# Down pass of a hybrid decoder trunk: later loads ordered behind one-column copies, first product's weights staged in the two general slots

## The chip, the cores and the metric

The kernel runs on one core of one Trainium2 chip. The metric is the device time of one execution in microseconds (us). The time before is 2121.87 us, the median of 3 runs (2121.12 to 2127.75). The engines are called by name: TensorE (PE; its weight loads are PEld), VectorE (DVE), ScalarE (ACT), GpSimd (POOL) and SyncE (SP). The last two issue most of the DMA loads and stores; SP also has "SPq", its queue, in the profile.

## The reference

Two residual layers over 1024 positions of width 1024. The first mixes with causal differential attention and causal pooling, the second with sliding-window attention; each ends with a gated MLP, and that is the part the change is in:

```python
def conv_glu_ffn(x, norm_g, w_up, conv_w, conv_b, w_down):
    S = x.shape[1]
    h = rms_norm(x, norm_g) @ w_up
    hp = jnp.pad(h, ((0, 0), (CONV_W - 1, 0), (0, 0)))
    c = conv_b
    for j in range(CONV_W):
        c = c + conv_w[j] * hp[:, j:j + S]
    gate, up = jnp.split(c, 2, axis=-1)
    return x + (jax.nn.silu(gate) * up) @ w_down
```

`w_down` is 2816 x 1024 in each layer. All inputs and outputs are float32.

## The kernel before

The activations are kept transposed (features on the 128 partitions, positions along the free side). For each layer the MLP has two passes. The **up pass** (`ffn_up`) computes the gated values for 22 blocks of 128 features and stores each block to a DRAM buffer `gd` (L393). The **down pass** (`ffn_down`, L547) reads `gd` back and multiplies it by `w_down`. It runs twice in the program, once in each layer.

The down pass is a product of 2 x 2 blocks done with seven block products instead of eight, in the order 1, 5, 6, 3, 7, 2, 4. Each product has K = 11 steps; a step is named (p, k), and `seq` (L554) lists them. A step takes a pair of operands, one of weights and one of `gd` values or sums of these. Each operand is split in a rounded high part (ScalarE, L131) and the rest (VectorE, L132), and a step is 4 x 3 = 12 matmuls of 128 x 512 (L634) into four PSUM banks. After the last step of each product VectorE adds the banks to the residual tiles `x` (L656).

A step's work is spread over three moments, counted in steps ahead of its matmuls. `fetch` (FETCH = 14 ahead) loads the weights from DRAM on SyncE's queue into staging tiles: two steps' worth in one load of 512 KB for products 1, 6, 3, 2 and 4 (L571), two loads of 256 KB for each step of products 5 and 7 (L578). `gather` (LEAD = 8 ahead) forms sums and differences on VectorE (L592). `prepare` (AHEAD = 3 ahead) splits both operands into `ws` tiles, of which there are 8, so four steps' operands.

The staging tiles come from pools with few slots: `wr` has 2, `x` has 8, `r` has 3. The `wr` and `x` slots are used by the up pass as well, and the 8 residual tiles of the down pass also live in `x` slots. The tiles `r` and `b` (11 of them) live in memory that the up pass used for other tiles. The table `stages` says which slots a product's loads take in turn. Before the change product 1, with 6 loads, takes `wr, wr, x, x, x, x`, and product 5 takes `r, wr, r, wr, r` in rotation.

The `gd` values come on GpSimd's queue. `b1` (4 tiles, L584) holds rows for the first EARLY = 4 steps of product 1; `b11` holds the others, and later all of them. The left half of each `b` tile is `b11[k]`, the right half `b21[k]`; the left and right halves of the tiles `cc`, which take `xg` slots, are `b12[k]` and `b22[k]`. The loads of `b11` (L673 for k of 4 and more, L676 for the first four), `b12` (L677), the residual `x` (L680), `b22` (L682) and `b21` (L684) are all written out before the first product. A tile framework orders the instructions of each engine by priority with a simulated timeline of its own, and puts in the semaphore waits that the tiles' uses demand; each engine and each queue then runs its instructions in that order.

Of the kernel before, what the change touches and what calls it, by code (L numbers as in the profile page):

```python
# [13 lines left out]
F32 = mybir.dt.float32  # L14
F32R = mybir.dt.float32r
I32 = mybir.dt.int32
AF = mybir.ActivationFunctionType
# [3 lines left out]
P = 128  # L21
D = 1024
S = 1024
ND = D // P
# [31 lines left out]
LO_OUT = 0  # L56
EARLY = 4
AHEAD = 3
LEAD = 8
FETCH = 14  # L60

PAR_NORM = 0
PAR_AQ, PAR_AK, PAR_SUB, PAR_CQ, PAR_CK = 32, 33, 34, 35, 36
# [5 lines left out]
class Trunk:  # L69
# [477 lines left out]
    def ffn_down(self, layer, xs, gd, after, begin=lambda part: None):  # L547

        nc, I = self.nc, self.I
        w = I["w_down"][layer]  # L550
        K = NF // 2
        lo, hi = slice(0, HALF), slice(HALF, S)
# [2 lines left out]
        pairs = {1: (0, lo), 6: (0, lo), 3: (K, lo), 2: (K, lo), 4: (K, hi)}  # L555
        raws, parts, ops = {}, {}, {}
        stages = {p: ("r", "wr", "r", "wr", "r") for p in (5, 6, 3, 7, 2)}
        stages[1], stages[4] = ("wr", "wr", "x", "x", "x", "x"), ("r",)
        taken = dict.fromkeys(stages, 0)

        def stage(p):
            t = self.big(stages[p][taken[p] % len(stages[p])], F32, HL)
            taken[p] += 1
            return t

        def fetch(p, k):
            if p in pairs:
                if k % 2 == 0:
                    t, n = stage(p), min(2, K - k)
                    off, cols = pairs[p]  # L570
                    nc.sync.dma_start(  # L571
                        t[:, :n, :], w[off + k:off + k + n, :, cols].rearrange("i p c -> p i c"))
                    raws[p, k], raws[p, k + 1] = t[:, 0, :], t[:, 1, :]
                return
            t = stage(p)
            first, second = ((k, hi), (K + k, hi)) if p == 5 else ((k, lo), (k, hi))
            for n, (row, cols) in enumerate((first, second)):
                nc.sync.dma_start(t[:, n, :], w[row, :, cols])  # L578
            raws[p, k] = t[:, 0, :], t[:, 1, :]

        g = lambda i, cols: gd[i * P:(i + 1) * P, cols]
# [5 lines left out]
        b11, b21 = [t[:, lo] for t in bb], [t[:, hi] for t in bb]  # L587
        b12, b22 = [t[:, lo] for t in cc], [t[:, hi] for t in cc]
# [6 lines left out]
        def operand(src):  # L595
            op = self.big("ws", F32R, HL)
            self.split2(src, op)
            return op

        def gather(p, k):  # L600
            r = raws.pop((p, k))
            with self.urgent(9000):
                if p == 1:
                    l, m = r, b1[k][:] if k < EARLY else b11[k]
                elif p == 5:
                    l = combine(sums[k], r[0], r[1], ALU.add)
                    m = combine(b11[k], b12[k], b11[k])
                elif p == 6:
                    l = combine(sums[k], sums[k], r)
                    m = combine(b11[k], b22[k], b11[k])  # L610
                elif p == 3:
                    l, m = combine(sums[k], r, sums[k]), b22[k]
                elif p == 7:
                    l = combine(r[0], r[0], r[1])
                    m = combine(b22[k], b22[k], b12[k])
                elif p == 2:
                    l, m = r, b21[k]
                else:
                    l, m = r, combine(b21[k], b21[k], b11[k])
            parts[p, k] = l, m  # L620

        def prepare(p, k):
            l, m = parts.pop((p, k))
            with self.urgent(12000):
                ops[p, k] = operand(l), operand(m)

        banks = {}

# [33 lines left out]
        def lead(n):  # L662
            if n + FETCH < len(seq):
                fetch(*seq[n + FETCH])
            if n + LEAD < len(seq):
                gather(*seq[n + LEAD])
            if n + AHEAD < len(seq):
                prepare(*seq[n + AHEAD])

        for n in range(FETCH):  # L670
            fetch(*seq[n])
        for k in range(EARLY, K):
            nc.gpsimd.dma_start(b11[k], g(k, hi))  # L673
        for k in range(K):
            if k < EARLY:
                nc.gpsimd.dma_start(b11[k], g(k, hi))  # L676
            nc.gpsimd.dma_start(b12[k], g(k, lo))  # L677
        x = [self.big("x") for _ in range(ND)]
        for d in range(ND):
            nc.gpsimd.dma_start(x[d][:], xs[d * P:(d + 1) * P, :])  # L680
        for k in range(K):
            nc.gpsimd.dma_start(b22[k], g(K + k, lo))  # L682
        for k in range(K):
            nc.gpsimd.dma_start(b21[k], g(K + k, hi))  # L684
        for n in range(LEAD):
            gather(*seq[n])
        for n in range(AHEAD):
            prepare(*seq[n])
# [755 lines left out]
```

## Time and profile before

| | |
|---|---|
| time, median of 3 runs | 2121.87 us (2121.12 to 2127.75) |
| profiled execution, its own time | 2124.41 us |
| span of its trace, first to last instruction | 2122.2 us |
| busy, share of the span: TensorE, its weight loads, VectorE, ScalarE, GpSimd | 95%, 81%, 75%, 52%, 12% |
| matmuls of the down passes (L634) | 1848 records in the trace |
| first and last of them | 850.8 us, 2117.7 us |
| DMA | 216.97 MB, 102 GB/s over the span |

The profile divides the span into 40 slices of 53 us; a digit is a busy share in tenths. The time of the trace counts from its first instruction. Matmuls overlap, so the duration of one (about 390 ns) is longer than the distance from one to the next. For an idle stretch the trace names what ended it, and "landing" of a DMA is the time from its issue until its data are in.

### The profile page before, as it was taken

Reading aid. Unit: us, or ns where it says so; the run is one execution under the profiler, and the core shown is the slowest. Engines: PE = TensorE matmul, PEld = TensorE weight load, DVE = VectorE, ACT = ScalarE, POOL = GpSimd, SP = SyncE. Lnnn points to the kernel's source line nnn. Section 1 sums busy time; section 2 is a strip of 40 time slices with the busy share of each in tenths; the row PEclk is TensorE's granted clock in tenths of the full one; section 3 lists DMA queues with packets and bytes.
Section 4 is the critical chain, followed back from the end, with each engine's and each line's share of the span. In section 5 each row is a group of like instructions: output and inputs, shape, how many; then the busy total and the mean of one; then the engine's idle time right before and its main releaser. Section 6 shows DMA issues by size and latency. Waiting matters only on the chain.

```text
span 2122.2 us, 28436 instructions
## 1 busy us (share of the span) xinstructions
PE 2016.3 (95%) x10440; PEld 1719.0 (81%) x10440; DVE 1602.0 (75%) x2882; ACT 1107.2 (52%) x2115; POOL 257.8 (12%) x449
## 2 busy tenths in 40 slices
PE   8999999889999999699999989999999999979999
PEld 6999877677888888588789988777788888867887
DVE  6677787877787777598863887777978777758975
ACT  5476755444455554345454875654645455433443
POOL 0322452000000002300013321200000000031000
PEclk9999999999999999899999999999999999999999
DMA  4210121302212224763431101212221222268342
GB/s 170 90 49 23 64 95 61 119 30 90 90 70 86 84 90 164 275 217 105 144 115 40 51 21 50 73 58 80 92 87 70 80 90 90 89 229 312 100 164 85
DMA packets 82333, 216.97 MB, mean 102 GB/s; under 512 B 9361, under 2 KB 9873, under 8 KB 82193
## 3 DMA queue, kind: packets, MB, share of 16 engines
q1 hardware_dynamic: 65296, 169.00, 23.0%
q0 software_dynamic: 9984, 33.56, 4.3%
q10 hardware_dynamic: 6912, 12.59, 1.6%
q8 instruction: 82, 1.34, 0.3%
q14 instruction: 59, 0.48, 0.1%
HBM read 173.17 MB, written 41.94 MB: 101 GB/s over the span
## 4 chain that ended last, share of the span: by engine, by line
PE 82%; DVE 7%; ACT 4%; DMA 3%; issue 2%; POOL 1%; SPq 0%; ACTq 0%; DVEq 0%; POOLq 0%
PE pss L372 22%; PE psq L372 12%; PE pss L634 7%; PE psq L634 6%; PE psd L720 6%; PE psd L123 5%; PE psd L372 5%; PE psd L634 4%; PE pss L720 3%; PE psq L123 2%; PE psq L893 1%; DMA b<-gd 1%; PE pss L945 1%; PE pss L791 1%; PE pss L792 1%
## 5 line engine op out<-in xcount | busy, mean ns | idle before, releaser
L372 PE MATMUL pss<-xg,ws 128*128 128x512 f32 x1248 | 297.0, 391 | 10.8 <-DVE xg L132 6.1
L372 PEld LDWEIGHTS pss<-xg,ws 128*128 128x128 f32 x1248 | 234.5, 189 | 62.3 <-DVE xg L132 7.0
L634 PE MATMUL pss<-ws,ws 128*128 128x512 f32 x726 | 209.5, 398 | 34.3 <-ACT ws L131 27.0
L372 PE MATMUL pss<-T,ws 128*128 128x512 f32 x912 | 224.6, 390 | 3.4 <-ACT ws L131 3.4
L372 PEld LDWEIGHTS pss<-T,ws 128*128 128x128 f32 x912 | 171.1, 188 | 39.6 <-ACT ws L131 4.2
L634 PEld LDWEIGHTS pss<-ws,ws 128*128 128x128 f32 x726 | 138.0, 192 | 66.1 <-ACT ws L131 27.9
L634 PE MATMUL psq<-ws,ws 128*128 128x512 f32 x660 | 191.5, 393 | 0.0
L720 PE MATMUL psd<-ws,xg 128*128 128x256 f32 x1344 | 184.0, 285 | 2.2 <-DVE hms L729 1.7
L720 PEld LDWEIGHTS psd<-ws,xg 128*128 128x128 f32 x1344 | 171.5, 191 | 4.7 <-DVE hms L729 2.3
L372 PE MATMUL psq<-xg,ws 128*128 128x512 f32 x696 | 168.5, 391 | 0.0
L132 DVE TENSOR_TENSOR ws<-hf,ws 128x512 fp32r<-128x512 f32 x160 | 109.6, 689 | 73.4 <-ACT ws L131 73.1
L372 PEld LDWEIGHTS psq<-xg,ws 128*128 128x128 f32 x696 | 131.1, 188 | 27.2
L131 ACT ACTIVATE ws<-wr 128x512 fp32r<-128x512 f32 (+1 forms) x156 | 114.2, 737 | 68.9 <-PE pss L372 23.7
L634 PEld LDWEIGHTS psq<-ws,ws 128*128 128x128 f32 x660 | 125.4, 190 | 26.4
L634 PE MATMUL psd<-ws,ws 128*128 128x512 f32 x462 | 145.6, 397 | 0.8 <-DVE ms L242 0.8
L123 PE MATMUL psd<-xg,ws 128*128 128x512 f32 x528 | 140.2, 404 | 3.1 <-DVE x L272 2.3
L131 ACT ACTIVATE ws<-hf 128x512 fp32r<-128x512 f32 x160 | 100.0, 630 | 76.1 <-PE psq L372 33.3
L677 POOL DMA_DIRECT2D xg<-gd x22 | 12.1, 552 | 988.8 <-PE pss L372 961.0
L132 POOL TENSOR_TENSOR ws<-wr,ws 128x1024 fp32r<-128x1024 f32 x38 | 95.0, 2506 | 284.8 <-ACT ws L131 242.3
L380 DVE SCALAR_TENSOR_TENSOR x<-x,conv,x 128x1023 f32<-128x1023 f32 x80 | 102.6, 1282 | 29.2 <-ACT x L379 28.9
L123 PEld LDWEIGHTS psd<-xg,ws 128*128 128x128 f32 x528 | 97.1, 192 | 23.2 <-DVE x L272 4.3
L372 PE MATMUL psq<-T,ws 128*128 128x512 f32 x456 | 115.6, 390 | 0.0
(263 smaller groups left out, 4071.1 us busy)
## 6 DMA issues: line engine op xcount, KB each, us to landing
wr<-in_dram SPq DMA_DIRECT2D x102, 512.0 KB, 3.5
x<-in_dram SPq DMA_DIRECT2D x44, 512.0 KB, 4.4
gd<-x SPq DMA_DIRECT2D x40, 512.0 KB, 2.6
r<-in_dram SPq DMA_DIRECT2D x64, 256.0 KB, 3.8
r<-in_dram SPq DMA_DIRECT2D x28, 512.0 KB, 3.8
xd<-x ACTq DMA_DIRECT2D x48, 256.0 KB, 2.2
xg<-gd POOLq DMA_DIRECT2D x44, 256.0 KB, 5.2
b<-gd POOLq DMA_DIRECT2D x44, 256.0 KB, 8.6
```

The costliest lines, as they stand in the source:

```text
L123: self.nc.tensor.matmul(out, a, b, start=(k == 0), stop=(k == n - 1))
L131: nc.scalar.activation(hi, raw, AF.Copy)
L132: (eng or nc.vector).tensor_tensor(out=lo, in0=raw, in1=hi.bitcast(F32), op=ALU.subtract)
L372: nc.tensor.matmul(bank[:], a, b, start=start and k == 0, stop=k == n - 1, skip_group_check=open)
L380: nc.vector.scalar_tensor_tensor(out=c[:, 1:], in0=hr[:, :S - 1], scalar=cw(1), in1=c[:, 1:], op0=ALU.mult, op1=ALU.add)
L634: nc.tensor.matmul(banks[p][m][:], l, r, start=opens and n == 0, stop=closes and n == 2, skip_group_check=p != 2)
L677: nc.gpsimd.dma_start(b12[k], g(k, lo))
L720: self.nc.tensor.matmul(out, a, m[:, d % 4, :], start=(n == 0), stop=(n == 23))
L791: nc.tensor.matmul(out, q[:, qs], his[m][:, ks], start=True, stop=False)
L792: nc.tensor.matmul(out, q[rows, qs], lo[rows, ks], start=False, stop=True)
L893: nc.tensor.matmul(po[:, :256], tt[:, kb * P:(kb + 1) * P], v, start=(b == 0 and t == 0), stop=(b == j and t == 1))
L945: nc.tensor.matmul(pu[:], a, b, start=d + n == 0, stop=d == ND - 1 and n == 2)
```

## The change

FETCH goes from 14 to 11 and LEAD from 8 to 5. Product 1 takes `wr` slots alone, so its six loads go through two slots in turn; product 5 takes `r, r, wr` in rotation.

The loads on GpSimd's queue are written in another order, and some wait. `b11` for k of 4 and more, all of `b12` and the first eight of `b22` are issued as before, without a condition. Each of the others is put on a list under a step: `ask(dst, src, when)`. When `prepare` has made that step's operands, `release` goes through the list. For each entry ScalarE copies one column of the step's first operand into the first column of the destination, and the load into that destination is written behind it. As the load overwrites the copied column, it has to wait for the copy, and the copy for the operand. The first four `b11` are under (1,4), the eight residual tiles under (1,5) to (1,8) and (5,1) to (5,4), the last three `b22` under (5,6) to (5,8), and `b21[k]` under (6,k): 26 loads in each pass.

```diff
--- before.py
+++ after.py
@@ -56,8 +56,8 @@
 LO_OUT = 0
 EARLY = 4
 AHEAD = 3
-LEAD = 8
-FETCH = 14
+LEAD = 5
+FETCH = 11
 
 PAR_NORM = 0
 PAR_AQ, PAR_AK, PAR_SUB, PAR_CQ, PAR_CK = 32, 33, 34, 35, 36
@@ -555,7 +555,7 @@
         pairs = {1: (0, lo), 6: (0, lo), 3: (K, lo), 2: (K, lo), 4: (K, hi)}
         raws, parts, ops = {}, {}, {}
         stages = {p: ("r", "wr", "r", "wr", "r") for p in (5, 6, 3, 7, 2)}
-        stages[1], stages[4] = ("wr", "wr", "x", "x", "x", "x"), ("r",)
+        stages[1], stages[5], stages[4] = ("wr",), ("r", "r", "wr"), ("r",)
         taken = dict.fromkeys(stages, 0)
 
         def stage(p):
@@ -623,6 +623,7 @@
             l, m = parts.pop((p, k))
             with self.urgent(12000):
                 ops[p, k] = operand(l), operand(m)
+            release(p, k)
 
         banks = {}
 
@@ -669,19 +670,31 @@
 
         for n in range(FETCH):
             fetch(*seq[n])
+        x = [self.big("x") for _ in range(ND)]
+        asked = {}
+
+        def ask(dst, src, when):
+            asked.setdefault(when, []).append((dst, src))
+
+        def release(p, k):
+            for dst, src in asked.pop((p, k), ()):
+                nc.scalar.activation(dst[:, 0:1], ops[p, k][0][:, 0, 0:1].bitcast(F32), AF.Copy)
+                nc.gpsimd.dma_start(dst, src)
+
         for k in range(EARLY, K):
             nc.gpsimd.dma_start(b11[k], g(k, hi))
         for k in range(K):
-            if k < EARLY:
-                nc.gpsimd.dma_start(b11[k], g(k, hi))
             nc.gpsimd.dma_start(b12[k], g(k, lo))
-        x = [self.big("x") for _ in range(ND)]
+        for k in range(K - 3):
+            nc.gpsimd.dma_start(b22[k], g(K + k, lo))
+        for k in range(EARLY):
+            ask(b11[k], g(k, hi), (1, 4))
         for d in range(ND):
-            nc.gpsimd.dma_start(x[d][:], xs[d * P:(d + 1) * P, :])
+            ask(x[d][:], xs[d * P:(d + 1) * P, :], (1, 5 + d) if d < 4 else (5, d - 3))
+        for k in range(K - 3, K):
+            ask(b22[k], g(K + k, lo), (5, k - 2))
         for k in range(K):
-            nc.gpsimd.dma_start(b22[k], g(K + k, lo))
-        for k in range(K):
-            nc.gpsimd.dma_start(b21[k], g(K + k, hi))
+            ask(b21[k], g(K + k, hi), (6, k))
         for n in range(LEAD):
             gather(*seq[n])
         for n in range(AHEAD):
```

## Rows read from the trace of the kernel before

**Rows 1.** The page: first TensorE's part of the line of busy times, then rows of the 40 slices (TensorE busy, its granted clock, DMA engines busy, all in tenths).

```profile
PE 2016.3 (95%) x10440; PEld 1719.0 (81%) x10440; DVE 1602.0 (75%) x2882; ACT 1107.2 (52%) x2115; POOL 257.8 (12%) x449
...
PE   8999999889999999699999989999999999979999
...
PEclk9999999999999999899999999999999999999999
DMA  4210121302212224763431101212221222268342
```

**Rows 2.** Stretches of the trace, matmuls of L634 alone. Columns: the stretch, its length, TensorE busy and number of matmuls, weight loads busy and their number, granted clock (1 is full), DMA share, GB/s. The first pass's rest of product 1 and then product 5, and the same of the second pass.

```profile
869.96:910.41 40.45, 23.72 (x85) 18.56 (x85) 0.79 1.03 387
910.41:940.50 30.09, 30.09 (x133) 24.67 (x132) 1.00 0.56 201
...
1897.83:1938.16 40.33, 23.30 (x85) 18.36 (x86) 0.79 1.02 384
1938.16:1968.30 30.14, 30.14 (x133) 24.69 (x132) 1.00 0.56 204
```

**Rows 3.** The timeline of TensorE in the first pass: start, length of the run, line, operands, number of matmuls, and in brackets the idle time before it and what ended it. Left out are runs without idle time before them.

```profile
869.35 0.61 PE L634 MATMUL psd<-ws,ws 128*128 128x512 f32 x2
883.46 1.22 PE L634 MATMUL pss<-ws,ws 128*128 128x512 f32 x2 [13.49 <-ACT ws L131]
...
888.62 0.62 PE L634 MATMUL pss<-ws,ws 128*128 128x512 f32 x2
...
895.11 1.95 PE L634 MATMUL pss<-ws,ws 128*128 128x512 f32 x4 [2.69 <-DVE ws L132]
...
898.56 0.69 PE L634 MATMUL pss<-ws,ws 128*128 128x512 f32 x2
...
903.00 1.20 PE L634 MATMUL pss<-ws,ws 128*128 128x512 f32 x4 [0.54 <-DVE ws L132]
```

**Rows 4.** The chain of work that ended last, in order of time, where it leaves TensorE in the first pass: start, length, what.

```profile
866.83 0.70 DVE xg L592
867.55 0.33 SPq L578
...
868.87 12.42 DMA x<-in_dram
881.31 19.05 DMA r<-in_dram
```

**Rows 5.** The timeline of SyncE's queue in the first pass: start, time over which the issues of the row lie, line, what is loaded or stored, number of DMAs.

```profile
846.91 11.05 SPq L578 DMA_DIRECT2D wr<-in_dram  x4
...
868.87 3.14 SPq L571 DMA_DIRECT2D x<-in_dram  x4
...
888.62 0.33 SPq L393 DMA_DIRECT2D gd<-x  x1
```

**Rows 6.** DMA from 864 to 912 us. The first two rows are the queues (q0 is GpSimd's, q1 SyncE's): packets, MB, share of the time of the 16 engines. The others are issues: number, KB each, median us to landing.

```profile
q0 software_dynamic: 3058, 10.36, 57.4%
q1 hardware_dynamic: 3659, 6.87, 39.3%
...
r<-in_dram SPq DMA_DIRECT2D x14, 256.0 KB, 11.2
...
x<-in_dram SPq DMA_DIRECT2D x3, 512.0 KB, 15.6
```

**Rows 7.** The same from 795 to 862 us, in the last part of the up pass: the loads of 512 KB into `wr` slots.

```profile
wr<-in_dram SPq DMA_DIRECT2D x2, 512.0 KB, 6.4
```

**Rows 8.** The timeline of GpSimd in the first pass: the last `b1`, the first of five loads into `xg` slots (they follow each other by 0.53 us), the first `b11`, and a residual tile.

```profile
838.53 0.54 POOL L584 DMA_DIRECT2D hf<-gd  x1
865.05 0.54 POOL L677 DMA_DIRECT2D xg<-gd  x1 [25.99 <-PE pss L372]
...
867.69 2.65 POOL L673 DMA_DIRECT2D b<-gd  x5
...
904.55 0.53 POOL L680 DMA_DIRECT2D x<-xd  x1 [8.07 <-DMA gd<-x]
```

**Rows 9.** From the views of single lines and tiles, the row of landings (least, median, greatest): L673 (`b11`), L677 (`b12`, first pass), and the loads into `r` tiles from 860 to 915 us, in this order.

```profile
DMA to landing us min/median/max: 6.7/8.3/9.0
...
DMA to landing us min/median/max: 2.8/5.1/7.4
...
DMA to landing us min/median/max: 7.7/11.2/20.6
```

**Rows 10.** The timelines of ScalarE and VectorE in the first pass (two rows of each: a split and the SiLU behind it; the last step of the convolution before that SiLU and a split), and a row of ScalarE's groups by shape with the mean of one in ns.

```profile
881.31 0.63 ACT L131 ACTIVATE ws<-x 128x512 fp32r<-128x512 f32 x1 [9.41 <-DMA x<-in_dram]
881.85 1.04 ACT L388 ACTIVATE x<-x 128x1024 f32<-128x1024 f32 x1
...
873.26 1.28 DVE L382 SCALAR_TENSOR_TENSOR x<-x,conv,x 128x1022 f32<-128x1022 f32 x1
...
884.06 0.69 DVE L132 TENSOR_TENSOR ws<-b,ws 128x512 fp32r<-128x512 f32 x1
...
L1310 ACT ACTIVATE warm<-warm 128x1 f32<-128x1 f32 x1 | 0.2, 203 | 0.0
```

**Rows 11.** Stretches of the trace, all instructions. Columns: the stretch, its length, busy time and number of instructions of TensorE, its weight loads, VectorE, ScalarE and GpSimd, granted clock, DMA share, GB/s.

```profile
869.96:910.41 40.45, 23.72 (x85) 18.56 (x85) 24.91 (x38) 13.49 (x22) 14.29 (x27) 0.79 1.03 387
910.00:980.00 70.00, 70.00 (x309) 57.73 (x308) 69.82 (x117) 29.66 (x52) 0.00 (x0) 1.00 0.44 153
980.00:1000.00 20.00, 20.00 (x90) 16.55 (x89) 14.52 (x24) 8.78 (x17) 0.10 (x1) 1.00 0.15 54
```

## The prediction

> **What bounds the kernel now.** I read the page first: TensorE is busy 95% of the span at a granted clock of 0.9 or more nearly everywhere, and its row has two holes, in slices 17 and 36, each beside the first saturated stretch of the DMA row [rows 1]. So the kernel is bound by TensorE except in two places, and both are the start of a down pass. The stretches by matmul line then give the size of a hole [rows 2]. In steady work 133 matmuls of the down pass take 30.09 us, a pace of 0.2262 us. From 869.96 to 910.41 us (the rest of the first product after its fourth step) only 85 are done in 40.45 us; at that pace they need 19.2 us, so **21.2 us** are lost, at a mean granted clock of 0.79. The second pass loses 40.33 - 19.2 = **21.1 us**. Together 42.3 us, 2.0% of the time, is all that this change can win at the start of the passes.
>
> What the hole is made of stands in TensorE's timeline [rows 3]: a stop of 13.49 us before step (1,4) that waits for ScalarE's split, then 2.69 us and 0.54 us that wait for VectorE. After the long stop the clock is at its lower level: 12 matmuls from 883.46 to 888.62 take 5.16 us instead of 2.71 (2.4 us lost); after the stop of 2.69 us, 8 matmuls from 895.11 to 898.56 take 3.45 us instead of 1.81 (1.6 us lost); after 0.54 us hardly anything.
>
> Why TensorE stops is in the chain and in SyncE's queue [rows 4, 5]. The weights of (1,4) to (1,10) go to x slots. Their loads stand in SyncE's queue behind two loads of product 5, which wait for VectorE at 866.83 us, so they go out from 868.87 us on, just when GpSimd's queue starts its own backlog. From there to 912 us the 16 DMA engines are full [rows 6]: the x staging loads need 15.6 us to land, the r loads 11.2, where a load of the first product in the quiet stretch before needed 6.4 [rows 7]. VectorE's second and third wait are for r loads in the same jam.
>
> **The change, part by part.** *Weights of product 1 in the wr slots.* A wr slot is free in the kernel before at 846.91 and again near 857 us: there the two loads of product 5 were issued [rows 5]. Now (1,4/5) and (1,6/7) go there; with the quiet landing of 6.4 us they are in by about 853 and 864 us, before TensorE runs dry at 869.96. This removes the 13.5 us as far as weights are the cause. Slot 0 comes free again once (1,4) and (1,5) are split, so (1,8/9) is issued at the latest near 875 us; at 6.4 us it lands at 881, at the 15.6 us of the jam at 891, and is due at 873 + 4 x 2.72 = 884. Cost 0 to 7 us, 0 taken, since the jam is what the other part thins out.
>
> *What is late next: b11[4].* The other operand of (1,4) is loaded by GpSimd. Its queue is in order and stood from 838.53 to 865.05 us behind a load into an xg slot that the up pass still read; five such loads later b11[4] went out at 867.69 [rows 8]. Two of the five (b22[8] and b22[9]) are now held back, 0.54 us each, so 866.6 us. Landing: the b loads took 6.7 to 9.0 us in the jam, the xg loads 2.8 at least and 5.1 in the middle [rows 9]. I take the middle of the xg loads, as the engines are not yet full at 866 us: landed 871.7, plus 1.3 us for ScalarE's and VectorE's split (0.63 and 0.69 us, [rows 10]) is a restart at 873.0. **TensorE still stops 3.0 us**; bounds 0.7 (2.8 us landing) and 8.0 (issue 867.7, 9.0 us). The clock falls as it did after 2.69 us: **1.6 us**; bounds 0 and 2.4.
>
> *Loads held back.* In front of GpSimd's queue stood 52 loads beside the four b1; 26 of them now wait for a copy: 4 of b11, 8 of x, 3 of b22, 11 of b21, together 18 x 0.262 + 8 x 0.524 = 8.9 MB. The hole moved 40.45 us x 387 GB/s = 15.7 MB [rows 2]. Not all of the 8.9 leaves the place: the copies of (1,4) to (1,8) free b11[0..3] and x[0..3] (3.1 MB) at about 872 to 884 us, near where they moved before. b21, x[4..7] and b22 (5.8 MB, 15 us of full engines) move to products 5 and 6, where the engines were about half busy [rows 11]. The later loads have their users far off: x[0..3] at the end of product 1 (some 8 us after the last copy), x[4..7] at the end of 5 (18 us or more), b22 in product 6, b21 in product 2: cost 0.
>
> *The copies.* 26 one-column ScalarE copies per pass at 0.2 us [rows 10] are 5.2 us on an engine that is about 40% busy here [rows 11]; nothing on the path. Each sits in ScalarE's queue before the next step's split, so a copy that waits for its slot holds splits up; see the third rival.
>
> *Product 5 and VectorE.* Its weights (0.524 MB a step, 2.72 us) share the engines with GpSimd's loads. In the jam GpSimd's queue took 57.4% of the engines and SyncE's 39.3% [rows 6], so SyncE gets about 157 GB/s of 387, 3.34 us a step: 0.62 us late a step while GpSimd is busy. GpSimd's 2.9 MB (x[4..7], b22) keep it busy for about 13 of the 30 us, a deficit of some 2.5 us, which the five staging tiles cover. [...] VectorE is tighter: it is busy 69.8 of the 70 us from 910 to 980 us [rows 11]. From 869.96 to 1000 us it works 24.9 + 69.8 + 14.5 = 109.2 us; if TensorE gets there some 15 us earlier there are 115 us, room for 5.8 us of idleness, where it idled 15.5 us in the hole. Some of its work is only running ahead (eight steps before, five now), so the need is less. I price the waits of TensorE on VectorE at what they are now, 2.69 + 0.54 = **3.2 us**; bounds 0 and 10 (the old 15.5 us of idleness less the room).
>
> *The rest.* LEAD 5 and FETCH 11 keep six steps between load and combine as before, and products 6, 3, 7, 2 and 4 keep their slots: 0.
>
> Sum for a pass: 21.2 - 3.0 - 1.6 - 3.2 = 13.4 us, 26.8 us for both. The profiled execution took 2124.4 us (span 2122.2 and 2.2 around it), which gives 2097.6; it lay 2.5 us over the median of the runs, so the forecast for the median is **2095 us**. Best: 21.2 - 0.7 = 20.5 a pass, 2081. With the upper bounds of b11 and clock and the same 3.2: 21.2 - 8.0 - 2.4 - 3.2 = 7.6 a pass, 2107.
>
> **Rivals.** *First: b11 stays late.* GpSimd keeps its order, and r loads and (1,8/9) fill the engines at once; b11[4] lands after 9.0 us and the restart is at 878: 2107 us by the sum above. For it speaks that the blocked queue is untouched; against it that nothing else is due then but 2 MB.
>
> *Second: VectorE becomes the bound.* Product 1 runs through, but the combines of product 5 wait for r loads as they did, and the 10 us come back in products 5 and 6: 21.2 - 3.0 - 1.6 - 10 = 6.6 a pass, 2109 us. For it: a VectorE full for 70 us. Against: part of that was catching up after the hole.
>
> *Third: a copy blocks ScalarE.* ScalarE works in order: at 881.31 us it had waited 9.41 us for a load, and the SiLU behind it (its input was ready at 874.5) ran at 881.85 [rows 10]. The copy for one of x[4..7] needs the slot whose store to gd went out at 888.62 us and was waited for until 904.55 [rows 5, 8]. If that store stays as late and the copy is reached at about 890, ScalarE stands 14.5 us; four prepared steps (10.9 us) cover most, so TensorE stops 3.6 us and loses 1.6 us of clock: 5.2 a pass more, 2105 us. Against it: the SiLU no longer stands behind a late load, so the store should be out by 880. [...]
>
> *Fourth: slower, product 5 starves.* It has three r and two wr slots. A tile that is occupied for T from load to combine gives a step of T / 5. The gain at the start is 21.2 - 3.0 - 1.6 = 16.6 a pass, and 11 steps eat it from T / 5 = 2.72 + 16.6 / 11 = 4.23, T = 21.1 us. The longest landing of an r load here was 20.6 us [rows 9]; with 2.4 us for VectorE's four operations of a step, T = 23, a step of 4.6, 20.7 us lost, net 4.1 slower a pass: 2130 us. Against it: the median landing in the jam was 11.2 us, and the jam ends sooner.
>
> *Fifth: it does not do what it says.* The copies come with the first steps, so the held loads start where they started, and TensorE restarts near 883 as before with only the second and third stop gone: 2.69 + 1.6 + 0.54 = 4.8, less 3 us of the first waits of product 5, about 2 a pass: 2118 us.
>
> **How the numbers follow.** Forecast (2081 to 2101) 0.58; b11 late 0.12; VectorE 0.09; ScalarE blocked 0.05; without effect 0.08; slower 0.08. A measurement tells 0.3%, 6.4 us, from no change. Faster is the first four, 0.84; same 0.08; slower 0.08. The range from 2081 to 2114 takes in the first four and leaves out the last two, 0.16.
>
> **What would show it.** Right: loads of product 1 in wr slots out at 847 and 857 us; TensorE's stop before (1,4) of 1 to 4 us, waiting for a split of b; product 5 starting near 897 instead of 910.4; DMA under 0.9 after some 890; 26 one-column copies of 0.2 us. Wrong: a stop of more than 5 us before (1,8) (weights, two slots too few), ScalarE idle behind a copy, VectorE idle for r loads in product 5 with TensorE waiting for it.

## The result and the profile after

The changed kernel takes 2107.41 us (median of 4 runs, 2104.91 to 2110.38); the kernel before took 2122.52 us beside it (4 runs, 2121.12 to 2127.75). The ratio is 0.9928, with the interval 0.9913 to 0.9943: faster by 15.1 us. The forecast was 2095 us in a range of 2081 to 2114, so direction and range held, and the gain is 0.56 of the 26.8 us that were summed up.

The page after, in two of the rows that answer to [rows 1]: the slices of TensorE and of the DMA engines.

```profile
PE   8999999889999999899999998899999999999999
...
DMA  4210122212222223673431101112212221268442
```

The two holes have gone from TensorE's row at this resolution. The DMA row keeps its peaks of 7 and 8 there. The stretches of the matmul line (L635 now) show how much of the loss is left: the rest of product 1 and the time of product 5, in both passes, to be held against [rows 2] (columns as there).

```profile
873.29:902.28 28.99, 22.87 (x85) 17.20 (x85) 0.88 0.93 340
902.28:934.40 32.12, 30.09 (x132) 24.26 (x131) 1.00 0.83 294
1889.76:1917.91 28.15, 22.76 (x84) 17.16 (x85) 0.88 0.94 347
1917.91:1949.00 31.09, 29.01 (x127) 23.34 (x126) 1.00 0.84 301
```

The rest of product 1 went from 40.45 to 28.99 us and from 40.33 to 28.15 us. Product 5, which ran without a stop before, now loses about 2 us in each pass. TensorE's timeline in the first pass says where; it answers to [rows 3], and times lie 3.3 us later than there, because the whole trace is that much late when the up pass ends (842.66 against 839.33 us at its third-last store). The first row is the last one before TensorE runs dry.

```profile
872.68 0.61 PE L635 MATMUL psd<-ws,ws 128*128 128x512 f32 x2
876.36 0.73 PE L635 MATMUL pss<-ws,ws 128*128 128x512 f32 x2 [3.06 <-ACT ws L131]
...
879.00 2.08 PE L635 MATMUL pss<-ws,ws 128*128 128x512 f32 x4 [1.44 <-DVE ws L132]
...
883.86 0.63 PE L635 MATMUL psd<-ws,ws 128*128 128x512 f32 x1
885.78 1.20 PE L635 MATMUL pss<-ws,ws 128*128 128x512 f32 x4 [1.29 <-DVE ws L132]
...
888.63 1.07 PE L635 MATMUL pss<-ws,ws 128*128 128x512 f32 x4
...
900.30 1.21 PE L635 MATMUL pss<-ws,ws 128*128 128x512 f32 x4 [0.18 <-DVE ws L132]
...
908.76 0.50 PE L635 MATMUL pss<-ws,ws 128*128 128x512 f32 x1 [0.86 <-ACT ws L131]
...
911.12 0.74 PE L635 MATMUL pss<-ws,ws 128*128 128x512 f32 x2 [1.17 <-DVE ws L132]
```

The stop of 13.49 us has become one of 3.06, but right behind it stand two more that VectorE ends, 1.44 and 1.29 us. Between these two the clock is at its lower level: four matmuls take 2.08 us from 879.00 on, where the granted clock is 0.50 until 884.49, and 1.07 us from 888.63 on, when it is up again at 1.00. The second pass has the same picture with stops of 2.87, 0.76, 1.28, 0.30, 0.19, 0.90 and 1.18 us.

DMA from 864 to 912 us, the queues and the landings of the `r` loads, to be held against [rows 6]:

```profile
q1 hardware_dynamic: 3653, 7.03, 41.9%
q0 software_dynamic: 1840, 6.29, 36.7%
...
r<-in_dram SPq DMA_DIRECT2D x15, 256.0 KB, 8.1
```

GpSimd's queue moves 6.29 MB here instead of 10.36, SyncE's as much as before, and an `r` load lands in 8.1 us instead of 11.2.

The span fell by 17.8 us. To see where, I cut both traces at four marks: the first and the third-last store of each up pass to `gd`, and the start of the fourth addition of product 3 in VectorE's timeline. Us, first and second pass where there are two:

| stretch | before | after | difference |
|---|---|---|---|
| start to first store | 471.8 | 475.0 | +3.2 |
| first to third-last store, both up passes | 367.5 and 365.7 | 367.7 and 365.6 | 0.0 |
| **third-last store to product 3 (start of the down pass)** | 163.52 and 162.79 | 154.44 and 153.10 | **-9.1 and -9.7** |
| product 3 to the first store of the second layer | 498.65 | 496.46 | -2.2 |
| rest | 92.2 | 92.2 | 0.0 |

So the change wins 18.8 us at the start of the two down passes. The rows beside it hold the attention parts and the up passes, which the change doesn't touch, and the rest of the down passes (products 7, 2 and 4). The sum of the third row, "the gain of the passes", is the measure of the experiments: it can be read from one trace, and it leaves out what moves elsewhere.

### The profile page after: what moved, and what is told of

Read it like the earlier page. It is cut to its first block, busy times and chain, and to the rows that moved or that the text cites. A ratio compares the mean times of both kernels' runs of the same rounds, so it can differ in the third digit from the quotient of the medians.

```text
span 2104.4 us, 28555 instructions
## 1 busy us (share of the span) xinstructions
PE 2014.0 (96%) x10440; PEld 1715.0 (81%) x10440; DVE 1604.5 (76%) x2882; ACT 1111.2 (53%) x2167; POOL 257.9 (12%) x449
## 4 chain that ended last, share of the span: by engine, by line
PE 81%; DVE 8%; ACT 5%; issue 4%; DMA 1%; POOL 1%; ACTq 0%; POOLq 0%; SPq 0%; DVEq 0%
PE pss L372 22%; PE psq L372 12%; PE pss L635 6%; PE psd L733 6%; PE psq L635 6%; PE psd L123 5%; PE psd L372 5%; PE psd L635 4%; PE pss L733 3%; PE psq L123 2%; PE psq L906 2%; PE pss L958 1%; PE pss L804 1%; PE psq L958 1%; PE pss L805 1%
## 5 line engine op out<-in xcount | busy, mean ns | idle before, releaser
L372 PE MATMUL pss<-xg,ws 128*128 128x512 f32 x1248 | 297.1, 391 | 10.8 <-DVE xg L132 6.1
L635 PE MATMUL pss<-ws,ws 128*128 128x512 f32 x726 | 207.2, 396 | 16.2 <-DVE ws L132 8.0
L635 PE MATMUL psq<-ws,ws 128*128 128x512 f32 x660 | 189.2, 391 | 0.0
L635 PEld LDWEIGHTS pss<-ws,ws 128*128 128x128 f32 x726 | 136.4, 190 | 50.5 <-DVE ws L132 12.5
L131 ACT ACTIVATE ws<-wr 128x512 fp32r<-128x512 f32 (+1 forms) x170 | 122.9, 727 | 87.3 <-DMA wr<-in_dram 25.0
L635 PEld LDWEIGHTS psq<-ws,ws 128*128 128x128 f32 x660 | 124.7, 189 | 26.2
L635 PE MATMUL psd<-ws,ws 128*128 128x512 f32 x462 | 142.2, 392 | 0.8 <-DVE ms L242 0.8
L687 POOL DMA_DIRECT2D xg<-gd x22 | 12.1, 551 | 985.7 <-PE pss L372 983.5
```

The lines of the kernel that those rows point to most:

```text
L131: nc.scalar.activation(hi, raw, AF.Copy)
L372: nc.tensor.matmul(bank[:], a, b, start=start and k == 0, stop=k == n - 1, skip_group_check=open)
L635: nc.tensor.matmul(banks[p][m][:], l, r, start=opens and n == 0, stop=closes and n == 2, skip_group_check=p != 2)
```

## The experiments

All ratios are against the kernel before, run beside them on the same chip. Gain of the passes in us, first + second, from one trace of each kernel; medians in us.

| run | gain of the passes | median | ratio, interval |
|---|---|---|---|
| the change | 9.1 + 9.7 | 2107.41 | 0.9928, 0.9913 to 0.9943 |
| weights_only | -0.8 + 0.1 | 2132.99 | 1.0041, 1.0027 to 1.0056 |
| hold_only | 5.5 + 6.3 | 2110.66 | 0.9941, 0.9922 to 0.9960 |
| lead_fetch_only | 0.3 - 1.2 | 2122.05 | 0.9990, 0.9978 to 1.0003 |
| b11_on_sync | 13.3 + 12.2 | 2106.57 | 0.9916, 0.9895 to 0.9937 |
| no_copies | -0.5 + 0.3 | 2133.78 | 1.0057, 1.0039 to 1.0075 |
| hold_b21_only | 4.7 + 4.8 | 2113.99 | 0.9957, 0.9943 to 0.9972 |
| diff5_on_gpsimd | 7.1 + 7.4 | 2115.26 | 0.9961, 0.9948 to 0.9975 |
| b11_sync_split_gpsimd | 13.1 + 12.2 | 2107.51 | 0.9929, 0.9913 to 0.9945 |
| after_again | 9.0 + 6.8 | 2106.59 | 0.9931, 0.9915 to 0.9947 |
| b11_sync_fetch12 | 12.1 + 12.8 | 2100.31 | 0.9899, 0.9880 to 0.9918 |
| b11_sync_tail_fetch12 | 11.5 + 11.3 | 2105.94 | 0.9919, 0.9904 to 0.9935 |
| no_last_convolution | 10.8 + 11.6 | 2102.14 | 0.9893, 0.9876 to 0.9911 |

The change was traced twice, and gained 18.8 and 15.8 us in the passes. A difference of some 3 us between two rows of this column is therefore not shown by it.

### The parts alone

**weights_only** is the kernel before with the new slots and the new LEAD and FETCH; nothing is held back.

```diff
-LEAD = 8
-FETCH = 14
+LEAD = 5
+FETCH = 11
...
-        stages[1], stages[4] = ("wr", "wr", "x", "x", "x", "x"), ("r",)
+        stages[1], stages[5], stages[4] = ("wr",), ("r", "r", "wr"), ("r",)
```

> The kernel before with the slots of products 1 and 5, LEAD and FETCH of the change, but no load held back and no copy. Theory (the stop before step (1,4) was the weights, and their new slots remove it): that stop falls from 13.5 us to 3 to 6 us, the waits on VectorE for r loads stay or grow in the jam; 8 to 14 us faster than the kernel before. Rival (the held-back loads bring the gain, the slots alone only move the weights in the same jam): 0 to 5 us faster.

The slots alone bring nothing in the passes; the longer time arises elsewhere, as the last section shows. TensorE's timeline of this kernel shows that the long stop is not gone but divided:

```profile
874.13 0.93 PE L634 MATMUL pss<-ws,ws 128*128 128x512 f32 x2 [4.72 <-ACT ws L131]
...
882.35 1.21 PE L634 MATMUL pss<-ws,ws 128*128 128x512 f32 x4 [2.69 <-DVE ws L132]
...
893.62 0.73 PE L634 MATMUL pss<-ws,ws 128*128 128x512 f32 x2 [3.68 <-ACT ws L131]
...
905.61 1.22 PE L634 MATMUL pss<-ws,ws 128*128 128x512 f32 x2 [4.61 <-ACT ws L131]
```

The first four stops are 15.7 us, and with 0.55 us more at 917 us the total is 16.3; before it was 16.7. The first is 4.72 us instead of 13.49, since the weights of (1,4) to (1,7) are in early. But slot 0 comes free only when they are split, the jam is still there, and the next two loads of product 1 land late in it. ScalarE's splits of (1,8) and (1,10) in its timeline:

```profile
892.42 0.63 ACT L131 ACTIVATE ws<-wr 128x512 fp32r<-128x512 f32 x1 [14.21 <-DMA wr<-in_dram]
...
904.40 0.63 ACT L131 ACTIVATE ws<-wr 128x512 fp32r<-128x512 f32 x1 [9.79 <-DMA wr<-in_dram]
```

The loads had been issued at 875.69 and 887.09 us, 16.7 and 17.3 us earlier. What is won at the first wait is given back at the next ones.

**hold_only** is the change with the slots of before (the `stages` line above taken back); LEAD and FETCH are the new ones.

> The changed kernel with the slots of products 1 and 5 of the kernel before (wr, wr, then x), so the copies, the held-back loads, LEAD 5 and FETCH 11 alone. Theory: the weights of (1,4) still go out near 869 us, but land in 6 us instead of 12; the stop before (1,4) is 6 to 9 us and the time 3 to 8 us below the kernel before. Rival (held-back loads are the gain): 12 us or more below, as fast as the changed kernel.

Holding back alone brings 11.8 us. One stop is left in the first pass, none behind it:

```profile
884.15 1.22 PE L635 MATMUL pss<-ws,ws 128*128 128x512 f32 x2 [13.67 <-ACT ws L131]
```

It is as long as it was. The weights of (1,4) again stand in SyncE's queue behind loads for product 5, and their landing is no quicker: ScalarE splits them at 881.67 us, 12.3 us after the issue, against 12.42 before [rows 4]. SyncE's timeline of this kernel:

```profile
868.06 0.80 SPq L578 DMA_DIRECT2D wr<-in_dram  x2
...
869.38 4.32 SPq L571 DMA_DIRECT2D x<-in_dram  x4
```

But the later stops, of 2.69 and 0.54 us before, are gone, and an `r` load lands in 9.0 us (median) instead of 11.2. Slots alone give -0.7, holding back alone 11.8, both 18.8 and 15.8 in the two traces: on top of the held loads the slots are worth 4 to 7 us, without them nothing.

**lead_fetch_only** has the two constants alone.

> The kernel before with LEAD 5 and FETCH 11 and nothing else. Theory: they keep six steps between load and combine and cost or bring nothing, within 3 us of the kernel before. Rival (less run-ahead of VectorE costs at the start of product 5): 4 us or more slower. Second rival: fewer loads of product 5 ahead of the x staging loads bring part of the gain, 4 us or more faster.

Nothing that can be measured.

**no_copies** is the change without the line that copies a column. The loads stand in the program where the change puts them, but wait for nothing.

```diff
-                nc.scalar.activation(dst[:, 0:1], ops[p, k][0][:, 0, 0:1].bitcast(F32), AF.Copy)
```

> The changed kernel without the one-column copies: the held loads are still written out behind the step that they are listed under, but wait for nothing of it. Theory (only the wait for the copy holds a load back; the place in the program does not): the loads of x and b21 go out as early as in weights_only, the first and fifth product end within 2 us of weights_only in each pass, and the time is 5 to 12 us above the kernel before. Rival (the place in the program is enough): as fast as the changed kernel, 12 us or more below the kernel before.

The gain is gone. Its trace shows the listed loads going out about as early as before, as soon as their tiles are free. GpSimd's timeline has the first `b21` load 48 us before the change lets it go (928.41 us):

```profile
880.49 0.54 POOL L681 DMA_DIRECT2D b<-gd  x1 [0.26 <-DMA b<-gd]
```

So the place in the program does nothing by itself; the true dependency does.

**hold_b21_only** lets all listed loads go at once but those of `b21`.

```diff
         def ask(dst, src, when):
+            if when[0] != 6:
+                nc.gpsimd.dma_start(dst, src)
+                return
             asked.setdefault(when, []).append((dst, src))
```

> The changed kernel with only the eleven b21 loads (2.9 MB a pass) held back by copies; x, the first b11 and the last b22 are issued at once. Theory (what counts is how many MB leave the first product, and b21 is half of the 5.8 MB that leave it): the two passes gain 8 to 14 us of the 18.8 that they gain with the whole change. Rival (the residual tiles x, 4.2 MB in loads of 512 KB, are what r and weights stand behind): under 5 us.

With 11 of 26 loads held (2.9 of 8.9 MB) the passes gain 9.5 us, half of the whole or a little more.

### The wait that is left at the seam

**b11_on_sync** puts the seven `b11` loads on SyncE's queue, past GpSimd's blocked one.

```diff
         for k in range(EARLY, K):
-            nc.gpsimd.dma_start(b11[k], g(k, hi))
+            nc.sync.dma_start(b11[k], g(k, hi))
```

> The changed kernel with the seven loads of b11 for steps 4 to 10 on SyncE's queue, past GpSimd's load that waits for an xg slot. Theory (what is late next is b11[4], and the clock falls for it): the stop of 3.1 us before (1,4) and the half clock behind it go, up to 5 us a pass; 6 to 10 us below the changed kernel. Rival (VectorE is the bound after the change, or the r loads that are now seven places later): the start is won and given back as waits on VectorE in product 5; within 3 us of the changed kernel.

The loads go out at 861.0 us and land in 5.0 to 5.9 us, before TensorE runs dry at 870.79. Yet TensorE stops:

```profile
873.29 0.73 PE L635 MATMUL pss<-ws,ws 128*128 128x512 f32 x2 [2.50 <-ACT ws L131]
...
874.69 1.19 PE L635 MATMUL pss<-ws,ws 128*128 128x512 f32 x4 [0.20 <-DVE ws L132]
```

ScalarE's timeline names the cause. The split of `b11[4]` stands in its queue behind the last convolution of the up pass (L379), which waits for the last block of that pass:

```profile
871.47 1.24 ACT L379 ACTIVATE x<-x,conv 128x1024 f32<-128x1024 f32 x1 [1.95 <-DVE x L496]
872.62 0.61 ACT L131 ACTIVATE ws<-b 128x512 fp32r<-128x512 f32 x1
```

So of the 3.06 us the late load had only 0.56 to itself; the rest lies under a second wait of nearly the same length. The passes still gain 6.7 us more than in the first trace of the change. In the first pass most of it is that the next stop is 0.20 us instead of 1.44, and that the clock doesn't fall there (four matmuls in 1.19 us, not 2.08). In the second pass the clock does fall behind a stop of the same 2.50 us: at 1889.85 us two matmuls take 1.22 us, not 0.73.

**b11_sync_split_gpsimd** adds to this that GpSimd splits the first `b11` operand, so ScalarE's queue is out of its way.

```diff
+                if p == 1 and k == EARLY:
+                    b = self.big("ws", F32R, HL)
+                    nc.gpsimd.tensor_copy(b[:, 0, :], m)
+                    nc.gpsimd.tensor_tensor(out=b[:, 1, :], in0=m, in1=b[:, 0, :].bitcast(F32), op=ALU.subtract)
+                    ops[p, k] = operand(l), b
...
```

> b11_on_sync with the split of step (1,4)'s gd operand on GpSimd instead of ScalarE and VectorE. Theory (with b11 early, the stop of 2.5 us that is left before (1,4) is ScalarE's queue, where the split stands behind the convolution of the up pass's last block): the stop falls under 1 us and the passes gain 3 to 5 us over b11_on_sync. Rival (the next step's split stands behind the same convolution): the stop moves to (1,5) and the passes gain 0 to 1 us.

GpSimd is done early, at 868.25 us, while TensorE runs dry at 869.25:

```profile
866.24 0.62 POOL L627 CAST ws<-b 128x512 fp32r<-128x512 f32 x1
866.95 1.30 POOL L628 TENSOR_TENSOR ws<-b,ws 128x512 fp32r<-128x512 f32 x1
```

But the stop is 2.61 us, as long as it was: the other operand's split stands behind the same convolution. ScalarE's timeline:

```profile
869.96 1.24 ACT L379 ACTIVATE x<-x,conv 128x1024 f32<-128x1024 f32 x1 [1.96 <-DVE x L496]
871.11 1.14 ACT L131 ACTIVATE ws<-wr 128x512 fp32r<-128x512 f32 x2
```

**b11_sync_tail_fetch12** moves that convolution's first step to GpSimd instead, with FETCH at 12.

```diff
-FETCH = 11
+FETCH = 12
...
-            nc.scalar.activation(c[:], hr[:], AF.Identity, bias=cw(3), scale=cw(2))
+            if last:
+                nc.gpsimd.tensor_scalar(c[:], hr[:], cw(2), cw(3), ALU.mult, ALU.add)
+            else:
+                nc.scalar.activation(c[:], hr[:], AF.Identity, bias=cw(3), scale=cw(2))
...
-            nc.gpsimd.dma_start(b11[k], g(k, hi))
+            nc.sync.dma_start(b11[k], g(k, hi))
```

> b11_sync_fetch12, with the first operation of the last convolution of each up pass (the one for the gate of block 21, which waits for the up pass's last product) on GpSimd instead of ScalarE. Theory (the stop before (1,4) that is left with b11 early is ScalarE's queue, where the split stands behind that convolution): the stop of 2.5 us falls to under 0.7 us in both passes, and the passes gain 3 to 5 us over b11_sync_fetch12. Rival (VectorE's part of the same convolution then stands before the splits' second half): the stop is 1.5 us or more and the gain under 2 us.

ScalarE's wait is gone: the first four matmuls of (1,4) run without a stop. A longer one comes behind them.

```profile
873.84 0.61 PE L638 MATMUL pss<-ws,ws 128*128 128x512 f32 x2
...
880.69 2.08 PE L638 MATMUL pss<-ws,ws 128*128 128x512 f32 x4 [5.78 <-DVE ws L132]
```

VectorE stands in the same way as ScalarE did. ScalarE's half of the two splits was done by 873.78 us, but VectorE has the convolution's next steps ahead of the second half, and now they wait for GpSimd, whose step takes 2.15 us; the second half starts at 879.95:

```profile
876.95 1.28 DVE L383 SCALAR_TENSOR_TENSOR x<-x,conv,x 128x1023 f32<-128x1023 f32 x1 [1.10 <-POOL x L380]
...
879.95 0.69 DVE L132 TENSOR_TENSOR ws<-b,ws 128x512 fp32r<-128x512 f32 x1
```

**b11_sync_fetch12** is the version without that move: the `b11` loads on SyncE's queue and FETCH 12. **after_again** is the change once more, on the same chip.

> b11_on_sync with FETCH 12 instead of 11. In the order of instructions that results, the second up pass starts with its statistics after 15 of its matmuls, as in the kernels before and after, where b11_on_sync has them after 24. Theory (b11_on_sync lost 5.8 us there, in a stop of 4 to 5 us that has nothing to do with the down pass): the passes gain 24 to 27 us over the kernel before, the stop at the start of the second up pass is 1.5 us again, and the time is 20 to 27 us below the kernel before. Rival (the time of attention swallows it anyway): as b11_on_sync, 17 us below.

> The changed kernel once more, for a second trace of it beside the next two. Theory (the passes gain the same 18 to 19 us each time, and what the time moves besides is attention, which differs from one execution to the next): passes 18 to 19.5 us below those of the kernel before, time 12 to 18 us below. Rival (the change costs something in the first layer's attention, whose end came 3 us later in the first trace of it): that end is 3 us late again.

The passes gain 24.8 us against 15.8 for the change on this chip (in its second pass the third stop is 2.26 us with a fall of the clock, where the first trace has 1.28 without, and there is a late one of 1.69), and the medians differ by 6.3 us, 2100.31 to 2106.59. It has the lowest median of all, 20.9 us below the kernel before, though the two intervals just touch. Its stops in the first pass are 2.50, 2.00 and 1.16 us, so the wait at the seam is still there.

**no_last_convolution** was to ask whether the convolution at the seam is all that is left. It is b11_sync_fetch12 with the convolution, the SiLU and the gate product of block 21 left out; the raw product is stored in their place.

> b11_sync_fetch12 without the convolution, the SiLU and the gate product of block 21 in each up pass: that block's values are stored as the up pass has them, so that part of the computation is left out. Theory (with b11 early, what holds the stop before (1,4) is the convolution of the up pass's last block, on ScalarE ahead of the first half of the split and on VectorE ahead of the second): in both passes no stop before (1,4) is over 1 us where b11_sync_fetch12 has 2.5 and 2.0 (1.1), and the passes gain 3 to 5 us over it. Rival (the stop is the loads: b11 or the r load that a combine waits for ahead of the split): a stop of 2 us or more is left within the first two steps after (1,3).

It doesn't answer the question. Without the convolution the last store stands ahead of the `b11` loads in SyncE's queue, they go out at 870.14 us, and the stop is 6.48 us, by data this time:

```profile
876.53 0.63 ACT L131 ACTIVATE ws<-b 128x512 fp32r<-128x512 f32 x1 [8.34 <-DMA b<-gd]
```

In the second pass the stop is 5.19 us. Whether TensorE would run through without that tail stays open.

### VectorE

**diff5_on_gpsimd** is the change with product 5's difference of two `b` tiles on GpSimd, which takes one of VectorE's operations from each step.

```diff
-                    m = combine(b11[k], b12[k], b11[k])
+                    m = combine(b11[k], b12[k], b11[k], eng=nc.gpsimd)
```

> The changed kernel with product 5's eleven differences of gd values on GpSimd instead of VectorE (11 x 0.6 us less for VectorE in a pass). Theory (VectorE, full from 895 to 970 us, sets the stops of 0.9 and 1.2 us at the start of product 5): these stops go, 2 to 4 us a pass, so 4 to 8 us below the changed kernel. Rival (the stops come from r and wr loads that are late, and VectorE only passes them on): within 2 us of the changed kernel in the passes, or slower, as GpSimd's queue with the held loads now waits behind the differences.

The passes gain 14.5 us, which is less than in either trace of the change (18.8 and 15.8), but against the second by less than the two differ. In the first pass, the stops of the change (3.06, 1.44, 1.29, 0.18, 0.86, 1.17) become 3.74, 0.77, 1.62, 0.27, 1.16, 1.61 and 1.48 us. A difference takes GpSimd 1.29 us at least, where VectorE needs 0.68, and GpSimd's queue also carries the held loads: six differences, 8.86 us from 894.35 on, stand ahead of the residual load at 903.15 us. So this way of unloading VectorE brings nothing. Part of the 7.9 us by which the median is above that of the change arises elsewhere, as the last section shows. Whether VectorE's load or its order sets the small stops isn't told apart by it.

## Why the prediction was right, and where its sum was off

**The time lies in the range, but not in the main case.** The main case was 2081 to 2101 us, with a chance of 0.58. The measured 2107.41 is at the figures of the first three rivals (2107, 2109 and 2105), and none of them came whole: `b11` cost 3.06 us and not 8, the stops for VectorE were 4.9 us a pass and not 10, and no copy blocked ScalarE.

**The bound and the hole: right.** All of the gain in the passes lies where the prediction looked, between the end of the up pass and product 5, and the hole was 21.2 us. From the rows after, the rest of product 1 still loses 28.99 - 85 x 0.2262 = 9.8 us in the first pass: 6.0 in four stops, 3.8 in clock and small gaps. Product 5 loses 2.0 in two stops.

**The weights: the mechanism was half right, and the credit wrong.** Their loads went out where they were forecast, into the two slots freed in the up pass (SyncE's timeline after, the first row; 847 and 857 us plus the shift of 3.3). The next one, (1,8/9), is the last row:

```profile
850.24 10.49 SPq L571 DMA_DIRECT2D wr<-in_dram  x2
...
879.57 0.38 SPq L571 DMA_DIRECT2D wr<-in_dram  x1
```

The step "this removes the 13.5 us as far as weights are the cause" credits the slots, and the (1,8/9) load was set at "Cost 0 to 7 us, 0 taken, since the jam is what the other part thins out". weights_only shows that without the held loads this cost eats the whole gain. With them the load still took 12.7 us (ScalarE's split at 892.27), nearer to the 15.6 of the jam than to the quiet 6.4. On the clock of before it was in at 888.9 us, and it was due at 884. TensorE hardly stopped for it (0.30 us in the second pass, less in the first) only because its other stops and the lower clock had made it about as late. So the 0 came out right by luck, and the losses don't simply add: without the others TensorE would have stood here. In b11_on_sync, where the others are shorter, it does. TensorE's and ScalarE's timelines of that kernel, at step (1,8):

```profile
886.36 0.73 PE L635 MATMUL pss<-ws,ws 128*128 128x512 f32 x2 [1.11 <-ACT ws L131]
...
885.16 0.63 ACT L131 ACTIVATE ws<-wr 128x512 fp32r<-128x512 f32 x1 [7.20 <-DMA wr<-in_dram]
```

**b11[4]: the size was right, the reason only in part.** Forecast 3.0 us, measured 3.06 and 2.87. The chain of the changed kernel has the landing that was estimated at 5.1 us:

```profile
870.27 5.38 DMA b<-gd
```

Issue at 870.27 is 866.9 on the clock of before, against 866.6 forecast; GpSimd's queue had stood 25.44 us as ever. But the prediction didn't look at what stands ahead of the split in ScalarE's queue. In the changed kernel that is this (ScalarE's timeline):

```profile
873.99 1.24 ACT L379 ACTIVATE x<-x,conv 128x1024 f32<-128x1024 f32 x1 [1.95 <-DVE x L496]
875.14 0.47 ACT L681 ACTIVATE b<-ws 128x1 f32<-128x1 f32 x4
875.68 0.63 ACT L131 ACTIVATE ws<-b 128x512 fp32r<-128x512 f32 x1
```

The convolution ends at 875.23, the load lands at 875.65. Between them ScalarE runs the four copies of step (1,4), until 875.61; they cost nothing here only because the load wasn't in yet. The lower bound of 0.7 us, and with it the best case of 2081, could not be had by an early load: with the load early (b11_on_sync) 2.50 us stay.

**The clock: mis-sized, 1.6 forecast, some 2.8 measured; small gaps of 1.0 were not in the sum.** Together they are the 3.8 us that the stops leave over. The price was that of the stop of 2.69 us, with 8 slow matmuls behind it [rows 3]. In the first pass 12 are slow: from 879.00 until 884.49 us they take 5.49 us instead of 2.71, at a granted clock of 0.50. The fall came behind the second of two stops, 3.06 and 1.44 us. But a pair is not needed for it. In the second pass of the change it came right behind the first stop (granted clock 0.50 from 1892.63 to 1894.30 us):

```profile
1892.63 1.22 PE L635 MATMUL pss<-ws,ws 128*128 128x512 f32 x2 [2.87 <-ACT ws L131]
```

**VectorE: mis-sized, 3.2 forecast, 4.9 measured.** The stops that it ends, and the one of 0.86 us where ScalarE waited for its combine, are 1.44 + 1.29 + 0.18 + 0.86 + 1.17 = 4.94 us. They are of two kinds. The stop of 1.29 us, and that of 1.28 in the second pass, is the old wait for an `r` load that was priced. VectorE stands for the load with a combine of product 5, and the split that TensorE needs is behind it:

```profile
882.69 0.69 DVE L592 TENSOR_TENSOR xg<-r 128x512 f32<-128x512 f32 x1 [3.15 <-DMA r<-in_dram]
...
885.04 0.69 DVE L132 TENSOR_TENSOR ws<-b,ws 128x512 fp32r<-128x512 f32 x1
```

The other 3.65 us are its queue, which was not priced: the convolution's tail ahead of the first splits, and then combines and splits of products 1 and 5 together. Between 900 and 910 us it is busy for all 10.00 us.

With these three sizes the sum of a pass is 21.2 - 3.1 - 3.8 - 4.9 = 9.4 us, and the traces have 9.1 and 9.7. So the 8.0 us between 26.8 and 18.8 are the clock with the small gaps (2.2 a pass) and VectorE (1.7 a pass). Of the other 3.7 us, from 18.8 to the 15.1 of the medians, 3.0 come from which executions were traced: the one before took 1.9 us more than its median (2124.41 against 2122.52), the one after 1.2 us less (2106.25 against 2107.41). The rest lies in the stretches beside. They vary from trace to trace: the one ahead of the first store came later by 3.2 us here and by 3.8 in b11_sync_tail_fetch12, but by 0.2 in hold_only, and earlier by 1.2 in b11_sync_fetch12.

**Held loads, copies, LEAD and FETCH: right at nothing.** The held loads go out after their steps and land well before their users. GpSimd's timeline: the `b11` loads behind the blocked queue, one of the residual tiles, and the first of `b21`.

```profile
868.38 1.90 POOL L687 DMA_DIRECT2D xg<-gd  x3 [25.44 <-PE pss L372]
870.27 3.71 POOL L685 DMA_DIRECT2D b<-gd  x7
...
894.33 0.53 POOL L682 DMA_DIRECT2D x<-xd  x1 [11.36 <-DVE ws L132]
...
928.41 0.54 POOL L682 DMA_DIRECT2D b<-gd  x1 [7.62 <-ACT b L681]
```

Waits of 7 to 11 us stand in front of them, and nobody waits for what they bring. The 52 copies take 0.19 us each, as forecast; ScalarE stands behind one for 1.25 us at most (the third rival). The fourth rival, product 5 starved, shows in no run: in weights_only too the long stops are those of product 1, the last of them before (1,10), and 0.55 us follow. The fifth, that the held loads start where they started, is what no_copies does, and there the passes take as long as before.

**Product 5's share of the engines: an estimate from [rows 6].** The prediction gave SyncE 157 of the 387 GB/s from its 39.3% against 57.4%, and had the five staging tiles cover the deficit of 2.5 us that follows. The split differs from kernel to kernel: from 864 to 912 us SyncE's queue has 40% of the bytes of the two queues in the kernel before ([rows 6]), 31% in weights_only and 53% in the changed kernel (7.03 MB to 6.29). By the profile's count GpSimd's packets are larger: in weights_only, 11.54 MB in 3392 packets against 5.09 MB in 2733 are 3.4 KB and 1.9 KB a packet. What sets the split, and whether both queues had work all the time, no run here shows. The sum didn't rest on it.

The queues of weights_only from which this is worked out, 864 to 912 us:

```profile
q0 software_dynamic: 3392, 11.54, 63.4%
q1 hardware_dynamic: 2733, 5.09, 28.6%
```

## What to carry to other kernels

When transfers jam at a seam, find the ones that nobody needs yet and give them a true dependency on the step after which they may go; a later place in the program changed nothing here (no_copies: a gain of -0.2 us in the passes), where the framework decides the order. Freeing slots for the urgent loads paid here only once the jam was thinned out (-0.7 us alone, 4 to 7 on top of the held loads), so measure such parts together and apart. When the data are early, read what stands ahead in the queues of the compute engines at the same seam: a tail of the stage before can hide behind the late load, with a stop of nearly the same length (2.50 us in b11_on_sync, 3.06 in the change).

## What the runs showed that was not expected

What a stop costs in clock can't be read from its length. The stop of 2.69 us before brought the clock to its lower level (four matmuls in 1.95 us, [rows 3], at a granted clock of 0.52 from 895.11 to 898.56 us); one of the same 2.69 us in weights_only left it at the upper one (four in 1.21 us, shown above). A stop of 2.50 us before (1,4) left it at the upper level in the first pass of b11_on_sync and brought it down in the second pass of the same kernel. What else the engine did before each of these stops wasn't varied.

An edit in the down pass moved instructions far away. At the start of the second layer's up pass, the first matmul to the first store takes 49.6 us in the kernels before and after and in b11_sync_fetch12, and 55.3 to 56.4 us in weights_only, no_copies, b11_on_sync, diff5_on_gpsimd and b11_sync_split_gpsimd, with a longer stop in TensorE's timeline (the first row is of weights_only, the second of the change):

```profile
1485.45 1.65 PE L372 MATMUL pss<-xg,ws 128*128 128x512 f32 x3 [4.57 <-DVE xg L132]
```

```profile
1469.70 0.96 PE L372 MATMUL pss<-xg,ws 128*128 128x512 f32 x3 [1.54 <-DVE xg L132]
```

In the same five kernels the second up pass takes 367.5 to 367.9 us from its first to its third-last store, where the kernel before takes 365.7. Together these 7.6 to 9.1 us are most of what weights_only and no_copies lose to the kernel before (9.4 and 11.2 us) with passes about as long as its own. They also keep b11_on_sync, with 25.5 us the largest gain of the passes, from having the lowest time.
